# Token-major gates for the 'b' heads, rotary work first on GpSimd, and probability transposes in pairs

## The chip, the cores and the metric

The kernel runs on one core of one Trainium2 chip. The metric is the device time of one execution in microseconds; the median of several runs is given. A core has five engines with an instruction stream each: TensorE (PE in the profile, its weight loads PEld), VectorE (DVE), ScalarE (ACT), GpSimd (POOL) and SyncE (SP), which here issues nearly all DMAs.

## What is computed

One encoder layer over 1024 tokens of width 1024, in float32 accuracy. One projection gives the queries, keys, values and gates of two groups of eight heads of width 64: group 'a' is neighbourhood attention over a 16 x 64 grid, group 'b' is windowed attention with two key heads, rotary positions and a learned sink.

```python
h = jnp.einsum('bsd,de->bse', x, w_in[layer])
q_a, k_a, v_a, z_a, q_b, k_b, v_b, z_b = jnp.split(h, SPLIT_POINTS, axis=-1)
y_a = neighborhood_attention(q_a, k_a, v_a, rel_bias)          # shapes left out
qb, kb = rotary(q_b, positions), rotary(k_b, positions)
y_b = windowed_gqa_with_sink(qb, kb, v_b, sink)                # |i - j| <= 128
mixed = jnp.concatenate([y_a * jax.nn.silu(z_a), y_b * jax.nn.silu(z_b)], axis=-1)
y = jnp.einsum('bse,ed->bsd', mixed, w_out[layer])
x = layer_norm(DEEPNORM_ALPHA * x + y, ln_gain[layer], ln_bias[layer])
```

## The kernel before

**Accuracy from half precision.** Large products are made of float16 pairs. A matrix is split into a high part (rounded to float16, on ACT) and a low part (the rest, on GpSimd or DVE), and a product is three passes: high by high, high by low, low by high. A weight block therefore costs an ACT instruction (line 199) and two of GpSimd (lines 204 and 205) before TensorE can use it. `w_split(m)` orders this for the m-th half block of four rows of tiles; `w_ops[m]` is its last operation.

**Stages.** First the values are projected (lines 411 to 661). Then come 21 projections of 128 columns each, named in `ORDER`: `q`, `k`, `z` for pairs 0 to 3 of 'a' heads, `qb`, `zb` for those of 'b' heads, and `kb`. Each works in two halves of 512 tokens, 24 matmuls of 512 columns a half, with the weights as the stationary operand (`project`, line 379); its result is feature-major: features on partitions, tokens along the row. The first six (`NPRO`) run alone, from about 59 to 122 us. The other 15 are the list `fill`, spread in between the attention. Last come the output projection (line 1031; a part of it is in `fill` too) and the normalisation (`final`).

**The attention** walks through 128 units, one per step: 64 of 'b' (pair p, head j, block of 128 queries), then 64 of 'a'. A unit takes its scores (`stage_qk`, lines 816 and 817 on PE, 826 on DVE), the exponentials (`stage_exp`, line 842 on ACT), one step later the split of the probabilities (`stage_tr`, line 852 on ACT, 853 on DVE) into one of six `split` tiles and a DMA transpose from there into one of nine `tr` tiles (line 856, on SP). Four units are a quad. From six steps after a quad's last scores on, `stage_pv` multiplies its transposed probabilities with the values (line 881), 33 or 36 matmuls of 64 columns; `stage_on` divides by the sums (line 890); after the second head of a pair `stage_ot` turns the result into the feature-major form with four PE transposes (line 901), and DVE multiplies it into the gate (line 904 for 'b', 910 for 'a').

**Gates.** `evac` writes the gates into tiles `zt[e]`: with Silu on ACT for the first three of `ORDER` (line 338), with Tanh on ACT and a product on DVE for the others (lines 341 and 342). `m_queue(e)` splits the gated result of 'b' pairs (`e` 4 to 7) into `mh` and `ml` (lines 1013 on ACT, 1014 on GpSimd) from the steps `M_AT` on; `m_split` does so for 'a' in `final`.

**What sets the order.** All is written out by hand. Work that isn't part of a step waits in four queues, one per engine, as `Op`s with a priority and dependencies. `pop` takes the next ones whose dependencies were emitted in an earlier step (two steps earlier where the dependency is a DMA on SP), the lowest priority number first: two of GpSimd's in each step (`NP`), one or two of ACT's and DVE's, one of SP's. `need` emits an operation at once where the next instruction requires it. `pump_to` emits as many matmuls of `fill` as belong to the step. An engine works through what is emitted for it strictly in order.

**The rotation** (`rope`): ACT copies, DVE shuffles (line 312), and then three operations of 128x512 (lines 313 to 315), on DVE in the first six projections and on GpSimd later. `split_q` and `split_k` make the high and low parts of the rotated result (lines 259 and 265); `split_k` also copies both parts of a key head to the other 64 partitions (line 295, GpSimd).

Of the kernel before, what the change touches and what calls it, by code (L numbers as in the profile page):

```python
# [15 lines left out]
S = 1024  # L16
# [11 lines left out]
LTT, LPP, BP, BH, BR, ND, NA, NX, F1 = 1, 6, 2, 9, 5, 1, 1, 6, 0.2  # L28
NSPLIT, NP = 6, 2
ORDER = ["zb0", "z0", "zb1", "kb", "qb0", "z1", "qb1", "zb2", "qb2", "k0", "qb3", "zb3", "q0", "k1", "q1",  # L30
# [6 lines left out]
ZTAG = {"z3": "zv", "zb3": "zc", "z2": "zs", "zb1": "zd", "zb2": "ze"}  # L37
# [9 lines left out]
WO_SCALE = 55  # L47
M_AT = [105, 112, 118, 120]
# [13 lines left out]
def hybrid_block(ctx, tc, xT, x, wt, wv, wo, bias, sink, gain, lbias, cos, sin, bmask, out):  # L62
# [83 lines left out]
    class Op:  # L146
        def __init__(self, eng, fn, deps, prio):
            self.eng, self.fn, self.deps, self.step = eng, fn, [d for d in deps if d is not None], None
            self.prio, self.born, self.lag = prio, clock["step"], 2 if eng == "sp" else 0
# [17 lines left out]
    def pop(eng, n, top=1, same=False):  # L167
        q = queues[eng]
        ready = [op for op in q if op.prio <= top and all(
            d.step is not None and d.step + d.lag < clock["step"] + (same and op.prio == 0 and d.eng == "act") for d in op.deps)]  # L170
# [112 lines left out]
    def split_k(p, half, src, dep=None):  # L283
# [3 lines left out]
        eng = "pool" if dep and clock["step"] is not None else "dve"  # L287
        for j in range(2):
# [4 lines left out]
            def dup_(w, j=j, a=a, o=o):  # L293
                t = own(w, p, j)
                nc.gpsimd.tensor_copy(t[o, sl], t[a, sl])  # L295
# [4 lines left out]
            dup = [enq("pool", lambda d=dup_: d("kh"), o1, after=32 if dep else 0),  # L300
                   enq("pool", lambda d=dup_: d("kl"), o2, after=36 if dep else 0)]
            stk_ops.setdefault((p, j, half), []).extend(dup)
        return ops

    def rope(ps, half):
# [7 lines left out]
        o3 = enq(eng, lambda: mul.tensor_mul(raw, raw, tiles["cos"][:, sl]), o2, after=3)  # L313
        o4 = enq(eng, lambda: mul.tensor_mul(sw, sw, tiles["sin"][:, sl]), o2, after=3)
        o5 = enq(eng, lambda: mul.tensor_add(raw, raw, sw), o3, o4, after=4)
        return raw, o1, o5

    def evac(name, half, ps):
# [22 lines left out]
        o = enq("act", lambda: nc.scalar.activation(zt[e][:, sl], ps, AF.Tanh, scale=half_inv), prio=0)  # L341
# [5 lines left out]
    def z_col(e):  # L347
        i = 0 if e in (4, 0, 5) else 1 if e == 1 else 2
        return zc[:, i:i + 1]
# [7 lines left out]

    def project(name):
        n = ORDER.index(name)
# [397 lines left out]
    split = [ap.tile([128, 3, 2, 128], F16, name=f"split{i}", bufs=1) for i in range(NSPLIT)]  # L757
# [87 lines left out]
    def stage_tr(u):  # L845
        g, p, j, t, _ = u
        n, ch = geom(u)
        pt = st.pop((u, "p"))
        c, m = ch[0], len(ch)
        hl = split[units.index(u) % NSPLIT]  # L850
# [474 lines left out]
```

## Time and profile before

| | |
|---|---|
| median of 3 runs (lowest to highest) | 446.54 us (446.23 to 446.97) |
| profiled execution: its time | 446.49 us |
| profiled execution: its span | 444.7 us |
| mean granted TensorE clock | 0.995 |
| busy: PE, DVE, ACT, POOL | 437.5, 344.2, 308.3, 221.6 us |

The span goes from the first to the last instruction of the profiled execution. A busy time is the time in which at least one instruction of an engine was under way. Matmuls overlap: a single one of 512 columns is recorded with 379 ns, so the distance between the starts of neighbours, which the chain of waits and the timeline give, says what one costs in a row.

### The profile page before, as it was taken

The page shows a single profiled execution, that of the slowest core. Times are in us where ns is not written, and L with a number is a line of the kernel's source. Part 1 is how long each engine was busy: PE and PEld are TensorE (multiplying, and loading weights), DVE is VectorE, ACT ScalarE, POOL GpSimd, SP SyncE. Part 2 cuts the span into 40 slices and gives each one's busy share as a digit, 9 for nine tenths or more (in the row PEclk, how much of TensorE's full clock was granted, in tenths as well). Part 3 has the DMA queues.
Part 4 walks back from the last instruction along what each step waited for, and adds up shares of the span by engine and source line. Part 5 has one row for each costly group of instructions (what it writes and reads, how often), then busy time and mean ns, then how long its engine had stood idle before and what let it go on. Part 6 is the DMA issues. An engine that isn't in the chain of part 4 may idle for free.

```text
span 444.7 us, 9505 instructions
## 1 busy us (share of the span) xinstructions
PE 437.5 (98%) x3289; PEld 255.5 (57%) x3289; DVE 344.2 (77%) x849; ACT 308.3 (69%) x700; POOL 221.6 (50%) x235
## 2 busy tenths in 40 slices
PE   9999999999999999999999999999999999999994
PEld 8997754444445565655565655656555654444453
DVE  5978967438986898887988888888878837589944
ACT  5759789766499988887868887888778946302401
POOL 0110074646839558866506767765574405205740
PEclk9999999999999999999999999999999999999997
DMA  8921469984659999587978899998999998103612
GB/s 272 390 91 60 145 235 339 336 292 169 213 127 214 206 190 181 98 162 143 164 127 175 169 182 180 213 170 213 192 204 253 167 172 347 55 0 102 232 69 72
DMA packets 133841, 81.39 MB, mean 183 GB/s; under 512 B 101280, under 2 KB 113440, under 8 KB 133536
## 3 DMA queue, kind: packets, MB, share of 16 engines
q1 hardware_dynamic: 133648, 80.64, 75.4%
q8 instruction: 26, 0.43, 0.4%
q14 instruction: 23, 0.19, 0.2%
q10 hardware_dynamic: 144, 0.13, 0.1%
HBM read 50.34 MB, written 9.96 MB: 136 GB/s over the span
## 4 chain that ended last, share of the span: by engine, by line
PE 91%; DMA 3%; POOL 3%; DVE 1%; issue 1%; ACT 1%; SPq 0%; POOLq 0%; DVEq 0%; ACTq 0%
PE ps_pj L379 44%; PE ps_s L1031 9%; PE ps_s L486 6%; PE ps_t L881 6%; PE ps_pj L1031 5%; PE ps_t L1031 5%; PE ps_s L816 4%; PE ps_s L817 4%; PE ps_pj L486 3%; PE ps_t L486 3%; DMA bias<-in_bias 3%; PE ps_t L901 1%; POOL wl L205 1%; PE ps_t L412 1%; POOL ks L295 1%
## 5 line engine op out<-in xcount | busy, mean ns | idle before, releaser
L379 PE MATMUL ps_pj<-xf,wh 128*128 128x512 f16 x672 | 202.1, 379 | 0.1
L379 PE MATMUL ps_pj<-xf,wl 128*128 128x512 f16 x336 | 127.3, 379 | 0.0
L379 PEld LDWEIGHTS <-wh 128*128 128x128 f16 x672 | 63.7, 98 | 60.4 <-DVE ks L263 0.5
L842 ACT ACTIVATE ps_s<-sn,nm 128x385 f32<-128x385 f32 (+3 forms) x128 | 70.1, 548 | 25.1 <-DVE nm L826 24.6
L853 DVE SCALAR_TENSOR_TENSOR split<-ps_s,split 128x384 f16<-128x384 f32 (+2 forms) x128 | 65.7, 513 | 27.5 <-ACT split L852 25.9
L1031 PEld LDWEIGHTS <-m 128*128 128x128 f16 x432 | 40.0, 98 | 41.1 <-DVE m L939 0.2
L852 ACT ACTIVATE split<-ps_s 128x384 f16<-128x384 f32 (+2 forms) x128 | 57.8, 452 | 2.5 <-DMA tr<-split 0.2
L204 POOL TENSOR_SCALAR wr<-wr,wsc 128x512 f32<-128x512 f32 x26 | 20.6, 791 | 68.1 <-ACT wh L199 61.6
L379 PEld LDWEIGHTS <-wl 128*128 128x128 f16 x336 | 32.9, 98 | 37.4
L826 DVE CUSTOM_DVE_ANT_0 sn<-ps_s,bm,nsk 128x384 f32<-128x384 f32 (+1 forms) x64 | 40.7, 636 | 2.0 <-PE ps_s L817 1.7
L1031 PE MATMUL ps_s<-wo,m 128*128 128x512 f16 (+1 forms) x192 | 40.8, 366 | 0.0
L816 PE MATMUL ps_s<-ks,qs 128*128 128x384 f16 (+4 forms) x128 | 39.2, 306 | 0.3 <-DVE qs L263 0.3
L817 PE MATMUL ps_s<-ks,qs 128*128 128x384 f16 (+4 forms) x128 | 39.2, 306 | 0.0
L826 DVE CUSTOM_DVE_ANT_0 sn<-ps_s,bias,sg 128x264 f32<-128x264 f32 (+1 forms) x64 | 35.0, 547 | 4.5 <-issue 1.5
L881 PEld LDWEIGHTS <-tr 128*128 128x128 f16 (+1 forms) x1104 | 36.6, 98 | 2.2
L205 POOL TENSOR_TENSOR wl<-wr,wh 128x512 f16<-128x512 f32 x26 | 32.7, 1257 | 2.2
L788 POOL TENSOR_SCALAR bias<-bias,rsg 128x552 f32<-128x552 f32 (+1 forms) x24 | 19.1, 797 | 23.8 <-DMA bias<-in_bias 22.6
L295 POOL COPY ks<-ks 64x512 f16<-64x512 f16 x40 | 26.0, 661 | 7.1 <-DVE ks L263 2.8
L1086 ACT ACTIVATE sd<-mv,eps 128x1 f32<-128x1 f32 x8 | 2.4, 295 | 36.5 <-DVE mv L1084 35.2
L1031 PE MATMUL ps_pj<-wo,m 128*128 128x512 f16 (+1 forms) x144 | 26.2, 326 | 0.0
L1130 POOL TENSOR_TENSOR xr<-xr,gb 128x512 f32<-128x512 f32 x7 | 9.8, 1396 | 32.4 <-ACT xr L1127 32.4
L842 ACT ACTIVATION_READ_ACCUMULATOR ps_s<-sn,nm 128x1 f32 x128 | 24.4, 190 | 0.0
(188 smaller groups left out, 813.8 us busy)
## 6 DMA issues: line engine op xcount, KB each, us to landing
ws<-in_wt SPq DMA_DIRECT2D x15, 512.0 KB, 5.9
wr<-in_wt SPq DMA_DIRECT2D x26, 256.0 KB, 3.6
wor<-in_wo SPq DMA_DIRECT2D x22, 256.0 KB, 3.5
bias<-in_bias SPq DMA_DIRECT2D x16, 276.0 KB, 3.3
xr<-in_x SPq DMA_DIRECT2D x8, 512.0 KB, 9.6
out<-xr SPq DMA_DIRECT2D x15, 256.0 KB, 2.1
bias<-in_bias SPq DMA_DIRECT2D x8, 368.0 KB, 3.8
wvraw<-in_wv SPq DMA_DIRECT2D x9, 320.0 KB, 5.8
```

Source lines behind the costliest of these rows:

```text
L205: nc.gpsimd.tensor_sub(l, raw, h)
L295: nc.gpsimd.tensor_copy(t[o, sl], t[a, sl])
L379: nc.tensor.matmul(ps, a[:, k % 4, :], mv, start=(k == 0 and i == 0), stop=(k == KT - 1 and i == 2))
L486: nc.tensor.matmul(ps[:, :320], lh[:, ts], rh[:, cs], start=(k == ko[0] and i == 0), stop=(k == ko[-1] and i == 2))
L816: nc.tensor.matmul(ps[:, :m], q, sl[0], start=True, stop=False)
L817: nc.tensor.matmul(ps[:, :m], q, sl[1], start=False, stop=True)
L826: nc.vector.tensor_tensor_reduce(sn[:, :m], ps[:, :m], bias_t, sg[:, c:c + 1], init, op0=ALU.add, op1=ALU.min, accum_out=nm)
L842: nc.scalar.activation(pt[:, :m], sn[:, :m], AF.Exp, bias=nm, scale=-1.0, accum_out=sm[:, k:k + 1])
L852: nc.scalar.activation(hl[:, :m, 0, :c], src, AF.Copy, scale=PSCALE)
L853: nc.vector.scalar_tensor_tensor(hl[:, :m, 1, :c], src, PSCALE, hl[:, :m, 0, :c], op0=ALU.mult, op1=ALU.subtract)
L881: nc.tensor.matmul(ps[:, HD * m:HD * m + HD], a, b_, start=(i == 0), stop=(i == len(mms) - 1))
L1031: nc.tensor.matmul(ps, lh[:, ts], rh[:, cs], start=(e == EO[0] and i == 0), stop=(e == EO[-1] and i == 2))
```

## The change

**Token-major gates of 'b'.** The projections zb0 to zb3 are done with tokens on partitions: `project_rows` takes the activations as the stationary operand and the weights as the moving one, in 96 matmuls of 128 columns for each half. `stage_on` then multiplies the normalised output with its scale in one DVE operation (`scalar_tensor_tensor`), and GpSimd multiplies it into the gate. `stage_ot`, with its four PE transposes and the product on DVE, remains for 'a' alone. The gated result of 'b' is split in the token-major form and turned by one DMA transpose for each half of 512 tokens, into the gate's own tile; no other tiles are taken for `m4` to `m7`. These splits are ordered at steps 26, 42, 57 and 86.

**Order.** zb2 and zb3 change places with z0 and z1: all four zb come in the first six projections.

**Rotation.** Its operations get priority 0.45, ahead of the weight splits' 0.5, and what GpSimd makes may be used by other engines a step later than before. The copies of the keys k0 are made by DMAs on SP.

**Pairs.** Two units share a `split` tile of double width (three in place of six single ones) and a `tr` tile (four in place of nine single ones). For 'b' one DMA transpose turns both units once the second one is split; 'a' has one for each unit, as before. The `gb` and `bb` tiles of the normalisation come from another pool.

```diff
-LTT, LPP, BP, BH, BR, ND, NA, NX, F1 = 1, 6, 2, 9, 5, 1, 1, 6, 0.2
-NSPLIT, NP = 6, 2
-ORDER = ["zb0", "z0", "zb1", "kb", "qb0", "z1", "qb1", "zb2", "qb2", "k0", "qb3", "zb3", "q0", "k1", "q1",
+LTT, LPP, BP, BH, BR, ND, NA, NX, F1 = 1, 6, 2, 4, 5, 1, 1, 6, 0.2
+NSPLIT, NP = 3, 2
+ORDER = ["zb0", "zb1", "zb2", "kb", "qb0", "zb3", "qb1", "z0", "qb2", "k0", "qb3", "z1", "q0", "k1", "q1",
...
-WO_SCALE = 55
-M_AT = [105, 112, 118, 120]
+WO_SCALE = 60
+M_AT = [26, 42, 57, 86]
+POP2_AT = (105, 112)
...
-            self.prio, self.born, self.lag = prio, clock["step"], 2 if eng == "sp" else 0
+            self.prio, self.born, self.lag = prio, clock["step"], {"sp": 2, "pool": 1}.get(eng, 0)
+
+        def behind(self, eng):
+            return 0 if self.eng == eng == "pool" else self.lag
...
+        to = "sp" if p == 0 and dep is None else "pool"
...
-                nc.gpsimd.tensor_copy(t[o, sl], t[a, sl])
+                if to == "sp":
+                    nc.sync.dma_start(t[o, sl], t[a, sl])
+                else:
+                    nc.gpsimd.tensor_copy(t[o, sl], t[a, sl])
...
-        o3 = enq(eng, lambda: mul.tensor_mul(raw, raw, tiles["cos"][:, sl]), o2, after=3)
+        o3 = enq(eng, lambda: mul.tensor_mul(raw, raw, tiles["cos"][:, sl]), o2, prio=0.45, after=3)
...
+    def project_rows(name):
+        n = ORDER.index(name)
+        w_split(2 * n + 2)
+        for half in range(2):
+            ps = new_group()
+            need(w_ops[2 * n], w_ops[2 * n + 1])
+            for c in range(96):
+                t, k, i = c // 24, c // 3 % 8, c % 3
...
+                ts = slice(128 * t, 128 * t + 128)
+                h, l = parts[2 * n + k // 4]
+                a, b = ((x16h, h), (x16l, h), (x16h, l))[i]
+                nc.tensor.matmul(ps[:, ts], a[half, k][:, ts], b[:, k % 4, :], start=(c % 24 == 0), stop=(c % 24 == 23))
...
-    split = [ap.tile([128, 3, 2, 128], F16, name=f"split{i}", bufs=1) for i in range(NSPLIT)]
+    split = [ap.tile([128, 6, 2, 128], F16, name=f"split{i}", bufs=1) for i in range(NSPLIT)]
...
+        if i % 2 == 0:
+            st["tr"] = ap.tile([128, 12, 128], F16, tag="tr", name="tr", bufs=BH)
+        tr = st["tr"]
+        if g == "a":
+            nc.sync.dma_start(tr[:, 2 * o:2 * o + 6, :], hl[:, o:o + 3].rearrange("p k i c -> p (k i c)"), transpose=True)
+            st[u, "tr"] = tr[:, 2 * o:]
+            return
+        if i % 2 == 0:
+            return
+        w = 2 * (len(sizes[0][1]) + len(sizes[1][1]))
+        nc.sync.dma_start(tr[:, :w, :], hl.rearrange("p k i c -> p (k i c)")[:, :128 * w], transpose=True)
...
-        nc.vector.tensor_mul(on[g, p, h][:, :, j, :], ps[:, :4 * HD].rearrange("p (m e) -> p m e", e=HD),
-                             ri.unsqueeze(2).to_broadcast([128, 4, HD]))
+        o, src = on[g, p, h][:, :, j, :], ps[:, :4 * HD].rearrange("p (m e) -> p m e", e=HD)
+        rb = ri.unsqueeze(2).to_broadcast([128, 4, HD])
+        if g == "a":
+            nc.vector.tensor_mul(o, src, rb)
+            return
+        nc.vector.scalar_tensor_tensor(o, src, z_col(4 + p), rb, op0=ALU.mult, op1=ALU.mult)
+        z = zt[4 + p].rearrange("p (t j e) -> p t j e", j=2, e=HD)[:, 4 * h:4 * h + 4, j, :]
+        gate_ops.setdefault(4 + p, []).append(enq("pool", lambda: nc.gpsimd.tensor_mul(z, z, o), prio=0.6))
...
-        if j == 0:
+        if j == 0 or g == "b":
             return
...
-        for h in (slice(0, 512), slice(512, S)):
-            o = enq("act", lambda h=h: nc.scalar.copy(mh[e][:, h], zt[e][:, h]))
-            m_ops[e].append(enq("pool", lambda h=h: nc.gpsimd.tensor_sub(
-                ml[e][:, h], zt[e][:, h], mh[e][:, h]), o))
...
+            o = enq("act", lambda hr=hr, z=z: nc.scalar.copy(hr[:, :, 0, :], z), *gate_ops[e])
+            o = enq("pool", lambda hr=hr, z=z: nc.gpsimd.tensor_sub(hr[:, :, 1, :], z, hr[:, :, 0, :]), o)
+            m_ops[e].append(enq("sp", lambda hr=hr, out16=out16: nc.sync.dma_start(
+                out16, hr.rearrange("p t i f -> p (t i f)"), transpose=True), o))
...
-        gb, bb = gain_tile[0], zslot("bb")
+        gb, bb = gain_tile[0], big_tile("bb", (128, D), F32)
...
-            enq("sp", gain_load, *m_ops[4])
+            enq("sp", gain_load)
```

99 lines of the change are left out of this document (62 added, 37 removed).

## The prediction

> **What bounds the kernel now.** I read the page first, its engine line and the slices.
>
> ```profile
> span 444.7 us, 9505 instructions
> PE 437.5 (98%) x3289; PEld 255.5 (57%) x3289; DVE 344.2 (77%) x849; ACT 308.3 (69%) x700; POOL 221.6 (50%) x235
> PE   9999999999999999999999999999999999999994
> DMA  8921469984659999587978899998999998103612
> ```
>
> PE is busy in every slice but the last; the DMA engines come next, near full from slice 10 to 33. Busy PE is not proof of PE at its peak, so I looked for pauses in the table by stage (PE, PEld, DVE, ACT, POOL busy; clock; DMA share; GB/s) and for the pitch of matmuls in the chain of waits (start, length, what).
>
> ```profile
> 140.00:160.00 20.00, 20.00 (x188) 11.53 (x187) 16.00 (x45) 18.72 (x51) 13.23 (x13) 1.00 1.09 186
> 240.00:260.00 20.00, 19.90 (x168) 11.16 (x165) 16.83 (x47) 16.45 (x44) 14.20 (x19) 1.00 0.84 161
> 320.00:340.00 20.00, 19.75 (x171) 11.03 (x169) 15.95 (x43) 16.78 (x44) 13.94 (x17) 1.00 1.12 210
> ...
> 68.72 10.38 PE ps_pj L379 x48
> 136.30 0.96 PE ps_t L881 x33
> 434.25 2.69 PE ps_pj L1031 x48
> ```
>
> 48 matmuls of 512 columns take 10.38 us, 216.25 ns each; 33 of 64 columns take 0.96, 29.1 ns each, every one with its own stationary operand; 48 of 128 columns take 2.69, 56.0 ns each. From about 1 us to the last matmul of the projection PE runs at these pitches at a granted clock of 1.00; the two stages shown are the only ones that lack more than a few hundredths (0.10 and 0.25 us). So a PE instruction removed is time won, one added is time lost, and a pause of PE, wherever it arises, lengthens the span by itself. Everything else counts only if it makes PE pause.
>
> **PE terms.** Removed: the four transposes of each finished 'b' head pair (line 901), eight calls in all.
>
> ```profile
> 164.84 0.60 PE L901 MATMUL ps_t<-identf,on 128*128 128x128 f32 x4
> 165.17 1.11 PEld L881 LDWEIGHTS <-tr 128*128 128x128 f16 x33
> 165.28 1.13 PE L881 MATMUL ps_t<-vb,tr 128*128 128x64 f16 x33
> ```
>
> From the first transpose (164.84) to the next matmul (165.28) is 0.44 us; 8 x 0.44 = 3.5 us less. They stand in PE's own order, beside no other PE work, so all of it is on the path.
>
> Changed: the eight halves of the zb projections. Each had 24 matmuls of 512 columns; token-major it has 96 of 128. Before: 192 x 216.25 = 41.52 us. After, at the 56.0 ns of line 1031, which also loads a fresh 128x128 operand for each: 768 x 56.0 = 43.01. That is +1.5 us.
>
> Against this stands a rule. The Trainium skill, page "TensorE: Matmul & The Clock Gate", section "Back-to-back issue gap", gives about 81 ns sustained for pairs of load and matmul at 128 columns and calls the 56 an isolated figure; by it the sum would rise by 768 x 81 - 41.5 = 20.7 us in place of 1.5. The trace disagrees over 48 such pairs in a row; no run here shows 192 in a row.
>
> First start: in the old order the second weight half is first needed for its low part after 14 matmuls of 512 columns; in the new one after 14 of 128.
>
> ```profile
> 59.27 1.16 POOL L205 TENSOR_TENSOR wl<-wr,wh 128x512 f16<-128x512 f32 x1
> 59.37 0.59 PE L379 MATMUL ps_pj<-xf,wh 128*128 128x512 f16 x2
> ```
>
> The low part is ready at 60.43; PE will ask for it at 59.37 + 14 x 0.056 = 60.15. A wait of 0.3 us, where there were 2 us of slack. Later zb projections find both halves split a whole projection (10.4 us) ahead: nothing.
>
> **Work off PE.** Nearest rows:
>
> ```profile
> L1099 POOL TENSOR_TENSOR xr<-xr,gb 128x256 f32<-128x256 f32 x1 | 0.7, 728 | 0.2 <-DVE stats L1080 0.2
> L295 POOL COPY ks<-ks 64x512 f16<-64x512 f16 x40 | 26.0, 661 | 7.1 <-DVE ks L263 2.8 <-ACT ks L257 1.5 <-DMA wr<-in_wt 0.6
> L1014 POOL TENSOR_TENSOR m<-z,m 128x512 f16<-128x512 f32 x8 | 9.1, 1161 | 3.8 <-ACT m L1013 3.8
> L904 DVE SCALAR_TENSOR_TENSOR z<-ps_t,zc,z 128x512 f32<-128x512 f32 x8 | 6.0, 747 | 0.0
> L890 DVE TENSOR_TENSOR on<-ps_t,ri 128x256 f32<-128x256 f32 x32 | 13.6, 424 | 2.6 <-PE ps_t L881 1.5
> L910 DVE SCALAR_TENSOR_TENSOR z<-ps_t,zc,z 128x256 f32<-128x256 f32 x16 | 7.0, 477 | 7.8 <-PE ps_t L901 7.8
> ```
>
> DVE loses 8 x 0.747 = 6.0 us and pays about 16 x (0.477 - 0.424) = 0.8 for the scaled normalisation. GpSimd gains 16 gate multiplications at about 0.73 (11.6 us) and loses 8 copies at 0.66 (5.3 us). The eight splits of the gated values (0.61 us on ACT, 1.16 on GpSimd) are not new: they move from steps 105 to 120, where ACT and GpSimd are short (the stage that lacks 0.25 us), to steps 26 to 86. All this hides behind PE, at nothing; without that cover it would cost its own length. The relief may return up to the 0.35 us that the two stages lack; I book none.
>
> The splits now end in eight DMA transposes of 128x1024 on SP. Their results are first wanted by the output projection from step 123 on, tens of steps later: nothing on the path. But each waits on SP for GpSimd, and the next unit's transpose is queued behind it; the emission gives it two steps of lag for that. The eight copies of k0 become small DMAs in steps 25 to 40, wanted at step 64: nothing. The gain and bias tiles no longer wait for gate tiles; PE does not pause in the output stage for what lies behind them: nothing.
>
> **Pairs.** A pair's one transpose leaves when the second unit is split and moves twice the bytes.
>
> ```profile
> 139.14 2.50 SPq L856 DMA_TRANSPOSE tr<-split  x2
> 142.93 1.12 PE L881 MATMUL ps_t<-vb,tr 128*128 128x64 f16 x33
> DMA to landing us min/median/max: 2.5/3.4/6.2
> L856 SPq DMA_TRANSPOSE tr<-split x128: 1188/1212/2615, 126.1 to 361.3; - x128
> 280.00:300.00 20.00, 20.00 (x167) 11.32 (x166) 17.40 (x47) 16.42 (x43) 13.65 (x17) 1.00 1.00 194
> ```
>
> Of the two transposes from 139.14 the first is the last of the second quad of units; it leaves at 139.14, its use begins at 142.93: 3.8 us for a median landing of 3.4. The pair's data is used from the 17th of 33 matmuls, 0.5 us later, so 4.3 us are there. Bounds: a pair lands like a single (3.4) or like two in a row (6.8). At full DMA load 194 GB/s passed, so 196.6 KB more are about 1.0 us (an estimate from that row): 4.4 us. And SP, which issued without a break there at 1.21 us each, has half as many to issue, and so issues up to 1.2 us earlier. I take 0.2 us of waiting in all, near the lower bound; the upper one is a rival.
>
> **Sum.** 446.49 (profiled execution: span 444.7 and 1.8 around it) - 3.5 + 1.5 + 0.3 + 0.2 = 445.0 us. The median of the runs shown, 446.54, lies 0.05 above that execution; I leave it out. A measurement of this kernel tells about 0.2%, 0.9 us, from no change.
>
> **Rivals.**
>
> *Pairs land late* (slower).
>
> ```profile
> 234.13 2.60 SPq L856 DMA_TRANSPOSE tr<-split  x2
> 239.04 1.12 PE L881 MATMUL ps_t<-vb,tr 128*128 128x64 f16 x33
> ```
>
> Place: the value products of the 'b' quads, above all those near 143 us, where the DMA share of the stage is 1.09, and near 239 us, where the last transpose of the quad (the second of the two, 236.73 - 1.21 = 235.5) leaves 3.5 us ahead of its use. It decides from a landing of 4.3 us on. At the upper bound, 6.8, PE waits 2.5 us; having waited, it has let ACT and DVE catch up, so I count it once at each place: 445.0 + 5.0 - 0.2 = 449.8. At a landing of 5.1 the two waits have eaten the gain (444.8 + 2 x 0.8 = 446.4), at 5.8 it is 447.8. For it: DMA near full. Against: SP's relief. 18%.
>
> *The rotated queries come late* (no change).
>
> ```profile
> 139.33 2.38 POOL L265 TENSOR_TENSOR qs<-rp_raw,qs 64x512 f16<-64x512 f32 x2
> 141.79 1.27 POOL L313 TENSOR_TENSOR rp_raw<-rp_raw,cos 128x512 f32<-128x512 f32 x1
> 147.89 0.27 PE L816 MATMUL ps_s<-ks,qs 128*128 128x256 f16 x1
> 133.00:151.00 18.00, 18.00 (x178) 10.51 (x177) 13.13 (x41) 16.53 (x45) 15.82 (x14) 1.00 1.09 212
> ```
>
> GpSimd is busy for 15.8 of these 18 us. The low parts of the queries (line 265) end at 141.7 and are wanted at 147.9. With the rotation of the other half ahead of them (3 x 1.27), one weight split (1.9), a gate (0.7) and a step of lag (1.6), they end at about 149.8, unless the step order lets them in between. A wait of up to 2 us; taken as 1.3: 446.3. GpSimd has rests of 0.5 and 0.7 us there and the rotation itself begins no later, so 12%.
>
> *The transposes were not what PE waited for* (slower). In that same stage ACT is busy for 16.5 of 18 us. If ACT sets the step, PE waits the removed 3.5 us elsewhere and only the costs stay: 446.5 + 2.0 = 448.5. Against it: PE does not pause there now, and DVE has less. 10%.
>
> *Weight loads bind in long runs* (slower).
>
> ```profile
> L881 PEld LDWEIGHTS <-tr 128*128 128x128 f16 x816 | 27.6, 98 | 1.7
> ```
>
> If each of the 768 loads took its 98 ns before its matmul, they would cost 75.3 us, 33.8 more than now: 446.5 - 3.5 + 33.8 = 476.8. The pitches of 29 and 56 ns speak against it: 3%. The 81 ns of the Trainium skill's page named above would be this case at half its price.
>
> **How the numbers follow.** The sum, 57%; its own range is 444.1 (the 0.35 us given back, no wait at the first start or at the pairs), rounded down to 444.0, to 445.6. Faster by over 0.2% is below 445.6: 57%. Within 0.2%: the late queries, and late pairs at a landing near 5, 12 + 8 = 20%. Slower: 10% of late pairs, 10 and 3: 23%. The range goes from 444.0 to 448.5; outside are the worst half of the late pairs, the weight loads and some 5% below.
>
> **What would show it.** Right: line 901 with 32 transposes; the zb matmuls at 56 ns; GpSimd's second low part ahead of the first zb half with PE idle about 0.3 us; PE busy without pauses from 120 to 430 us. Wrong: PE released by the pair's DMA at the value products; line 816 released by line 265; zb matmuls above 60 ns; an idle PE in stages that have none now.

## The result and the profile after

| | before | after |
|---|---|---|
| median (lowest to highest, runs) | 446.46 us (446.22 to 446.97, 6) | 450.97 us (449.63 to 454.07, 6) |
| ratio to before, 95% interval | | 1.0106 (1.0073 to 1.0138) |
| profiled execution: time, span | 446.49, 444.7 us | 450.65, 448.8 us |

The change makes the kernel about 1% slower: 4.5 us more, where 1.5 us less was forecast, and outside the range. The medians in this document leave out one execution, of experiment 11, which took 568.43 us at a mean granted clock of 0.752.

The page after: span, busy times, PE's slices, and the head of the chain of work that ended last.

```profile
span 448.8 us, 10466 instructions
PE 436.6 (97%) x3833; PEld 276.1 (62%) x3833; DVE 341.4 (76%) x841; ACT 308.1 (69%) x700; POOL 228.4 (51%) x240
PE   9999999999999999799999999999999899999995
...
PE 76%; DVE 7%; ACT 5%; POOL 4%; issue 4%; DMA 3%; SPq 0%; DVEq 0%; POOLq 0%; ACTq 0%
```

PE has two slices under 9 that were full before (the 17th, at 180 us, and the 32nd, at 350 us). The chain now passes through DVE, ACT, POOL and DMA for 19% of the span, where it was 8% before: PE waits for them more often. The table by stage (columns as in the prediction) says where, and its last row how much:

```profile
160.00:180.00 20.00, 19.35 (x161) 10.33 (x157) 16.35 (x47) 16.76 (x42) 15.47 (x15) 1.00 0.94 188
180.00:200.00 20.00, 17.67 (x174) 10.23 (x175) 15.99 (x47) 15.22 (x39) 13.73 (x15) 1.00 0.77 144
...
340.00:360.00 20.00, 18.82 (x193) 11.48 (x192) 15.24 (x45) 13.71 (x36) 2.33 (x3) 1.00 1.07 202
sum 240.00, PE 234.28 PEld 133.90 DVE 195.00 ACT 194.17 POOL 156.34; mean PE 19.52 PEld 11.16 DVE 16.25 ACT 16.18 POOL 13.03
```

The same stages of the kernel before:

```profile
sum 240.00, PE 239.64 PEld 137.54 DVE 199.14 ACT 197.44 POOL 148.40; mean PE 19.97 PEld 11.46 DVE 16.59 ACT 16.45 POOL 12.37
```

From 120 to 360 us PE lacks 5.7 us where it lacked 0.4. What it waits for, in the view of waits (engine, tile and line, releaser: us in total, times, longest):

```profile
PE ps_s L856 <- POOL qs L269: 3.0, 1, 3.0
...
PE ps_t L934 <- DMA tr<-split: 1.4, 3, 1.0
...
PE ps_s L856 <- DVE qs L267: 0.6, 1, 0.6
PE ps_pj L419 <- DVE ks L267: 0.5, 2, 0.3
PE ps_pj L419 <- DVE qs L267: 0.2, 1, 0.2
PE ps_pj L389 <- POOL wl L209: 0.2, 1, 0.2
```

(Line 856 was 816: scores; 934 was 881: value products; 419 was 379; 267 and 269 were 263 and 265: low parts of the feature-major results, and of the rotated ones; 389 is the matmul of `project_rows`.) Before, the same view had one such row of 0.3 us. Idle time is counted from the modelled end of the matmul before; by the distance of starts, less the pitch, a pause is a little longer. Summed that way from the first zb matmul to the last matmul of the output projection (before the change, from the first matmul of line 379), the pauses are 7.35 us after and 0.69 before. The rest of that stretch, PE's own work, is 374.71 us after and 376.65 before: 1.9 less, where 2.0 (-3.5 + 1.5) was forecast. The stretch begins 0.2 us later, and what follows it is 0.8 us shorter (7.2 us against 8.0). So 6.7 - 1.9 + 0.2 - 0.8 = 4.2 us, and the two spans (448.8 and 444.7) differ by 4.1; the medians differ by 4.5. The forecast of PE's work held, and new pauses made the loss.

**The 3.0 us pause** comes at unit 32, the first of pair 2, the third of the four pairs of 'b' heads. The timeline of PE:

```profile
178.97 0.38 PE L419 MATMUL ps_pj<-xf,wl 128*128 128x512 f16 x1
182.33 0.28 PE L856 MATMUL ps_s<-ks,qs 128*128 128x256 f16 x1 [2.98 <-POOL qs L269]
```

And what GpSimd did meanwhile, with one operation of DVE put ahead (start, length, engine and line, operation; in brackets idle time before it and releaser):

```profile
165.12 0.72 DVE L322 STREAM_SHUFFLE rp_sw<-rp_raw 128x512 f32<-128x512 f32 x1
...
163.75 0.72 POOL L952 TENSOR_TENSOR z<-z,on 128x256 f32<-128x256 f32 x1 [2.69 <-DVE on L950]
165.98 1.28 POOL L323 TENSOR_TENSOR rp_raw<-rp_raw,cos 128x512 f32<-128x512 f32 x1 [1.51 <-DVE sn L861]
...
171.70 0.72 POOL L952 TENSOR_TENSOR z<-z,on 128x256 f32<-128x256 f32 x1
172.39 2.27 POOL L1078 TENSOR_TENSOR hr<-z,hr 128x512 f16<-128x512 f32 x2
174.63 1.26 POOL L323 TENSOR_TENSOR rp_raw<-rp_raw,cos 128x512 f32<-128x512 f32 x1
175.85 1.26 POOL L324 TENSOR_TENSOR rp_sw<-rp_sw,sin 128x512 f32<-128x512 f32 x1
177.19 1.26 POOL L325 TENSOR_TENSOR rp_raw<-rp_raw,rp_sw 128x512 f32<-128x512 f32 x1
178.44 0.69 POOL L208 TENSOR_SCALAR wr<-wr,wsc 128x512 f32<-128x512 f32 x1
179.21 1.15 POOL L209 TENSOR_TENSOR wl<-wr,wh 128x512 f16<-128x512 f32 x1
180.32 0.73 POOL L952 TENSOR_TENSOR z<-z,on 128x256 f32<-128x256 f32 x1
181.12 3.60 POOL L269 TENSOR_TENSOR qs<-rp_raw,qs 64x512 f16<-64x512 f32 x3
```

The low part that unit 32 needs (line 269) stands last: behind the rotation of the other half (lines 323 to 325, 3.8 us), a weight split, a gate product (line 952), and the moved splits of gated values (line 1078, 2.3 us). At 163.75 a gate product has also held GpSimd still for 2.7 us, because it was emitted in the same step as the normalisation on DVE (line 950) that it needs. The pause at unit 32 did not grow by it: the rotation of the first half, behind this gate product, needs the shuffle on DVE (line 322), which ends at 165.84, and so GpSimd idled again until 165.98. From there to the low part GpSimd has no rest.

Two things set unit 32 apart from units 16 and 48, where PE doesn't pause. The queue from the first rotation (line 323) to the low part is 15.1 us long and not 13.2 or 13.1; the two splits of line 1078, 2.3 us, stand in it only here. And that rotation starts 13.2 us before PE wants the unit, and not 15.2 or 14.7.

### The profile page after: what moved, and what is told of

It reads as the page before. It is cut to its first block, busy times and chain, and to the rows that moved or that the text cites. A ratio compares the mean times of both kernels' runs of the same rounds, so it can differ in the third digit from the quotient of the medians.

```text
span 448.8 us, 10466 instructions
## 1 busy us (share of the span) xinstructions
PE 436.6 (97%) x3833; PEld 276.1 (62%) x3833; DVE 341.4 (76%) x841; ACT 308.1 (69%) x700; POOL 228.4 (51%) x240
## 4 chain that ended last, share of the span: by engine, by line
PE 76%; DVE 7%; ACT 5%; POOL 4%; issue 4%; DMA 3%; SPq 0%; DVEq 0%; POOLq 0%; ACTq 0%
PE ps_pj L419 27%; PE ps_pj L389 9%; PE ps_s L1096 9%; PE ps_s L526 6%; PE ps_t L1096 5%; PE ps_pj L1096 5%; PE ps_t L934 5%; PE ps_pj L526 3%; PE ps_s L856 3%; PE ps_s L857 3%; DVE split L896 2%; DMA tr<-split 2%; PE ps_t L526 2%; ACT split L895 1%; DVE qs L267 1%
## 5 line engine op out<-in xcount | busy, mean ns | idle before, releaser
L419 PE MATMUL ps_pj<-xf,wh 128*128 128x512 f16 x544 | 164.0, 379 | 0.7 <-DVE ks L267 0.5
L419 PE MATMUL ps_pj<-xf,wl 128*128 128x512 f16 x272 | 103.1, 379 | 0.0
L419 PEld LDWEIGHTS <-wh 128*128 128x128 f16 x544 | 51.3, 98 | 46.6 <-DVE ks L267 1.0
L419 PEld LDWEIGHTS <-wl 128*128 128x128 f16 x272 | 26.6, 98 | 30.0
L389 PEld LDWEIGHTS <-xf 128*128 128x128 f16 x768 | 43.2, 98 | 0.6 <-issue 0.3
L389 PE MATMUL ps_pj<-wh,xf 128*128 128x128 f16 x512 | 43.4, 219 | 0.0
L389 PE MATMUL ps_pj<-wl,xf 128*128 128x128 f16 x256 | 43.2, 219 | 0.2 <-POOL wl L209 0.2
L828 POOL TENSOR_SCALAR bias<-bias,rsg 128x552 f32<-128x552 f32 (+1 forms) x24 | 19.0, 794 | 33.8 <-DMA bias<-in_bias 22.1
L1096 PEld LDWEIGHTS <-m 128*128 128x128 f16 x216 | 20.2, 98 | 21.4 <-DVE m L998 0.2
L1096 PEld LDWEIGHTS <-z 128*128 128x128 f16 x216 | 20.0, 98 | 19.7
```

Source lines behind the costliest of these rows:

```text
L389: nc.tensor.matmul(ps[:, ts], a[half, k][:, ts], b[:, k % 4, :], start=(c % 24 == 0), stop=(c % 24 == 23))
L419: nc.tensor.matmul(ps, a[:, k % 4, :], mv, start=(k == 0 and i == 0), stop=(k == KT - 1 and i == 2))
L1096: nc.tensor.matmul(ps, lh[:, t, :], rh[:, cs], start=(e == EO[0] and i == 0), stop=(e == EO[-1] and i == 2))
```

## The experiments

The theory after the first reading: PE's terms are right, and the change adds three waits. GpSimd stands still in front of operations that wait for DVE, and has the wrong order; SP stands in front of the new DMA transposes until GpSimd is done; SP is full in the 'a' stage. The rival: the order of the whole is so tight that a pause taken away in one place comes back in another. Edits are against the kernel after, unless said otherwise; each ratio is to the kernel before, on the same chip. Numbers 12 to 15 ran as four together, in this order, and so did 6, 8, 17 and 18: that is what "the second of these four" and the like mean in the expectations.

### The order on GpSimd

**1. Rotation part undone** (priority and lag as before the change).

```diff
-self.prio, self.born, self.lag = prio, clock["step"], {"sp": 2, "pool": 1}.get(eng, 0)
+self.prio, self.born, self.lag = prio, clock["step"], 2 if eng == "sp" else 0
...
-o3 = enq(eng, lambda: mul.tensor_mul(raw, raw, tiles["cos"][:, sl]), o2, prio=0.45, after=3)
+o3 = enq(eng, lambda: mul.tensor_mul(raw, raw, tiles["cos"][:, sl]), o2, after=3)
...
```

> The changed kernel with its rotation part undone: the three GpSimd operations of the rotation have their old priority 1, and GpSimd's results may be used in the next step. Theory 'order': the 3.1 us pause before the scores of unit 32 comes from the order on GpSimd (the other half's rotation, one weight split and the gate splits ahead of the low parts of the queries, 8.7 us in the trace of the changed kernel). The low parts then follow the first half's rotation after one weight split and a gate product, so they end near 175 us, 4 us before they are wanted: no pause there, time 450.97 - 3.1 = 447.9 us. Theory 'load': the pause comes from the work that GpSimd was given in addition (gate products, splits at step 26); then the order changes little, at least 1.5 us of pause stay, and the time is 449.4 us or more.

Measured: 451.31 us, 1.0121 (1.0074 to 1.0168). A miss: the pause at unit 32 went, but PE then waited for DVE at the scores (2.8 us) and for DMAs at the value products (2.6 us). These waits are those of the profiled execution, which at 455.13 us is the longest of the four.

**2. Only the lag of GpSimd's results undone** (the first line of that diff).

> The changed kernel with one part of the rotation undone: GpSimd's results may be used in the next step again; the rotation keeps its priority of 0.45. Theory 'order': the other half's rotation (3.8 us) and a weight split (1.9 us) stay ahead of the low parts, but the gate splits (2.3 us) now come behind them, so the low part ends near 179.3 us and about 0.2 us of pause stay: time 448.1 us. Theory 'load': the work is the same, the pause stays above 1.5 us.

Measured: 450.69 us, 1.009 (1.0057 to 1.0123). The pause at unit 32 went: the low part still stands behind the other half's rotation, but now ahead of the splits of gated values and of a gate product, and ends at 178.7 us, just in time. Pauses at the value products of 'b' took its place. The timelines of SP and then of PE show where:

```profile
208.00 1.75 SPq L908 DMA_TRANSPOSE tr<-split  x1
214.28 1.23 SPq L1079 DMA_TRANSPOSE z<-hr  x1
215.62 1.40 SPq L908 DMA_TRANSPOSE tr<-split  x1
```

```profile
228.35 0.70 PE L934 MATMUL ps_t<-vb,tr 128*128 128x64 f16 x18 [1.84 <-DMA tr<-split]
```

SP ends an issue at 209.75 and then stands for 4.5 us in front of a transpose of gated values (line 1079), whose split GpSimd makes from 213.1 on; the next pair of units (line 908) is behind it. That pair was split by 211.1; it leaves 4.5 us late and lands at 219.15, and PE pauses 0.5 us for it. ACT waits for the same landing, because it needs the `split` tile again (1.0 us), and waits for the next one at 224.2 (1.3 us): the delay is handed on through the three tiles. The pair that PE misses at 228.35 itself left as soon as it was split (222.8) and took until 228.31 to land, so how much of the 1.84 us comes from SP's standing is not shown. In the kernel after no such pause is seen; PE comes 3 us later there.

**3. Only the priority of the rotation undone** (the rest of that diff).

> The changed kernel with the other part undone: the rotation has its old priority 1, the step of lag stays. Theory 'order': the gate splits (2.3 us) and a weight split (1.9 us) are ahead of the low parts, the other half's rotation is behind, so the low part ends near 177.8 us, 1.4 us early: no pause at unit 32, time 447.9 us. If the lag alone were the cause, the pause would stay at 3 us and the time near 451.

Measured: 455.18 us, 1.019 (1.0165 to 1.0214). The pause at unit 32 went, as the theory of the order had it, but the time is a miss: with the lag kept and the rotation behind the weight splits, the low part of the second half of the queries comes later still, and PE waits for line 269 once, 5.1 us, at unit 36. So the priority helps the rotation, but leaves the queries' splits behind it. Between the two profiled executions, this one and that of the kernel after, only 2.1 us of the 5.0 is more waiting; the rest goes with the granted clock (last section).

**4. Splits of the gated values later** (`M_AT = [36, 52, 66, 86]`).

> The changed kernel with the splits of the gated values of the first three 'b' pairs ordered ten steps later (steps 36, 52, 66 and 86 in place of 26, 42, 57 and 86); rotation as in the changed kernel. Theory 'order': 2.3 us of what is ahead of the low parts at unit 32 goes, 0.8 us of pause stay there, time 448.7 us, unless the splits find another place to be in the way. Theory 'load' gives the same at unit 32; with the runs that leave the work and change the order this tells how the 3.1 us divide.

Measured: 450.87 us, 1.0099 (1.0068 to 1.013). A miss: the pause is still 2.5 us. With the splits away GpSimd stands for DVE instead (0.9 us ahead of the rotation, 0.7 ahead of a gate product), and the low part begins at 180.3 in place of 181.1.

**5. Gate products two steps after their normalisation.**

```diff
-gate_ops.setdefault(4 + p, []).append(enq("pool", lambda: nc.gpsimd.tensor_mul(z, z, o), prio=0.6))
+made = Op("dve", None, [], 1)
+made.step = clock["step"] + 1
+gate_ops.setdefault(4 + p, []).append(enq("pool", lambda: nc.gpsimd.tensor_mul(z, z, o), made, prio=0.6))
```

> The changed kernel with one change: a gate product of GpSimd is emitted two steps after the normalisation (line 950) that makes its input, and not in the same step. In the trace of the changed kernel GpSimd stood 20.2 us in all in front of the gate products, waiting for DVE, with all its other work behind it. Theory 'GpSimd blocked': without these waits the rotation and the low parts of the queries are earlier by 2 to 3 us, the pause of 3.1 us before unit 32 goes, and as in the run with the old lag the value products of 'b' may then pause 1 to 3 us because the pairs' transposes leave late: 448 to 449.5 us. Theory 'load' (the added work itself): GpSimd still ends the low parts late, the pause stays above 1.5 us, time 449.4 us or more.

Measured: 449.02 us, 1.0051 (1.0034 to 1.0068). GpSimd's waits for the normalisation, after and here:

```profile
POOL z L952 <- DVE on L950: 20.2, 8, 6.8
```

```profile
POOL z L954 <- DVE on L950: 2.5, 1, 2.5
```

17.7 us of standing still are gone, but PE gains only about 2 us, and unit 32 still waits 1.7 us. Nor does this show that the standing made the pause. The rotation starts no earlier than in the kernel after (165.98), since it needs the shuffle:

```profile
166.04 1.28 POOL L323 TENSOR_TENSOR rp_raw<-rp_raw,cos 128x512 f32<-128x512 f32 x1 [4.21 <-DVE sn L861]
```

What got shorter is the queue: with their gate products later, the splits of gated values start at 182.4 in place of 172.4, behind the low part, which begins at 179.9 in place of 181.1. What the standing is worth by itself is not separated.

**6. Only the splits of the queries ahead of the rotation** (gate products as in the kernel after).

```diff
 def split_q(...):
-    prio = 0 if dep is None else 1
+    prio = 0 if dep is None else 0.4
```

> The changed kernel, in which only the splits of the queries go ahead of the rotation by priority (0.4 against 0.45) on ACT and GpSimd; the gate product stays behind the normalisation in the same step. Theory 'the order on GpSimd': the pause of 3.1 us at line 856 (unit 32) falls below 1 us; pauses at the value products of 'b' may appear instead, as they did whenever that pause went: 448 to 450. Rival 'the gate products block GpSimd': the pause stays at 1.5 to 3 us, since GpSimd still stands about 20 us in all: 450 to 451.

Measured: 448.01 us, 1.0042 (1.0027 to 1.0057); 3.0 us of the 4.5 come back with this number alone (it also orders the high parts on ACT). GpSimd in it:

```profile
172.53 2.29 POOL L1078 TENSOR_TENSOR hr<-z,hr 128x512 f16<-128x512 f32 x2
174.89 2.38 POOL L269 TENSOR_TENSOR qs<-rp_raw,qs 64x512 f16<-64x512 f32 x2
177.35 1.27 POOL L323 TENSOR_TENSOR rp_raw<-rp_raw,cos 128x512 f32<-128x512 f32 x1
```

Two low parts (line 269) now stand ahead of the other half's rotation and end at 177.3, and the pause at unit 32 is gone. GpSimd still stood 2.4 us for a normalisation at 163.9. The pause is thus shown to come from the order. Waits for DMAs at the value products took a part back: 2.6 us in place of 1.4.

### The queue of SP

**7. Pairs of 'b' undone** (`if g == "a":` becomes `if True:`).

> The changed kernel with the pairs undone: each unit of 'b' has its own DMA transpose again (the tiles stay double). Theory 'pairs help or are neutral': SP has 32 issues of 1.2 us more between 126 and 240 us, in front of which the transposes of the gated values wait too; 451 to 453 us. Rival 'pairs cause the loss': the time falls by 2 us or more, to 449 us or less.

Measured: 454.02 us, 1.0164 (1.0145 to 1.0183): 3.1 us slower than the kernel after. PE waits 3.9 us for DMAs at the value products, 2.5 more than in the kernel after. Not all of the 3.1 need be the pairs: the tiles stay double here (four `tr` tiles of two units in place of nine of one), and in the profiled execution the granted clock is 0.50 for 3.4 us after the pause at unit 32.

**8. Pairs alone, in the kernel before** (its `stage_tr` replaced by the new one; three double `split` tiles, four double `tr` tiles).

> The kernel before with the pairs alone: tiles of double width, one DMA transpose for two 'b' units, one each for 'a'; gates, order and rotation as before. Theory 'pairs cost nearly nothing': no pause at the value products of 'b' and a time within 0.5 us of the kernel before (446.1 to 447.1). Rival 'pairs land late': pauses at the value products near 143 and 239 us, 0.5 to 2 us each: 447.5 to 450.

Measured: 446.62 us, 1.0011 (0.9997 to 1.0025): no difference. PE nowhere waits for a pair. In the trace, an issue of SP for one unit of 'a' (line 862) and for a pair (line 868), lowest, median and highest ns:

```profile
L862 SPq DMA_TRANSPOSE tr<-split x64: 1209/1218/1883, 245.4 to 359.9; - x64
L868 SPq DMA_TRANSPOSE tr<-split x32: 1255/1427/2163, 127.0 to 242.6; - x32
```

Up to twice the data costs SP 17% more time, so pairs save SP two fifths.

**9. Token-major gates alone** (experiment 1's diff, and no pairs; the new order of the projections, the copies of k0 on SP and the double tiles stay).

> The changed kernel with the rotation part undone (priority and lag of GpSimd's results as before) and one DMA transpose for each unit: of the change stay the token-major gates with their splits and DMA transposes, and the order of the projections that belongs to them. Theory 'the gates bring new work to GpSimd and SP, whose waits cost more than the 2.0 us that PE saves': slower than the kernel before by 5 to 9 us, 451.5 to 455.5, with pauses at the scores and at the value products. Rival 'the loss comes from the new order of the rotation': 445 to 447, near the prediction's sum.

Measured: 457.81 us, 1.0268 (1.0236 to 1.0299): 11.2 us slower, more than either theory gave. What PE waits for most in it:

```profile
PE ps_t L934 <- DMA tr<-split: 8.1, 7, 1.5
PE ps_s L856 <- DVE split L896: 2.1, 3, 1.3
```

And SP:

```profile
184.02 1.80 SPq L1079 DMA_TRANSPOSE z<-hr  x1
185.94 1.22 SPq L902 DMA_TRANSPOSE tr<-split  x1
187.20 0.58 SPq L301 DMA_DIRECT2D ks<-ks  x1
188.26 1.35 SPq L902 DMA_TRANSPOSE tr<-split  x1
189.72 1.24 SPq L1079 DMA_TRANSPOSE z<-hr  x1
```

SP stands in front of the first transpose of gated values until 184, and then goes from one issue to the next: the transposes of the units, those of the gated values, and the eight copies of k0 that the change gave it. An issue, which ends 1.3 us after its unit is split when SP is free, ends 7.1 us after it at 210.5 us, and still 4.3 at 241.2. Against experiment 1, which has the same gates and old rotation but pairs, the pairs are worth 457.8 - 451.3 = 6.5 us. In this change they pay for the gates.

**10. 'a' units in pairs too** (the `if g == "a"` block is left out). In the kernel after, the last split of gated values falls into the 'a' stage. Its SP there, and PE later:

```profile
292.95 1.23 SPq L1079 DMA_TRANSPOSE z<-hr  x1
294.29 1.31 SPq L902 DMA_TRANSPOSE tr<-split  x1
295.69 1.26 SPq L1079 DMA_TRANSPOSE z<-hr  x1
```

From here on SP is behind: its issues end up to 6.9 us after their split, where in this stage of the kernel before it is up to 5.4.

```profile
357.31 0.44 PE L934 MATMUL ps_t<-va,tr 96*128 96x64 f16 x9 [0.95 <-DMA tr<-split]
```

> The changed kernel with one change: the units of 'a' too are turned in pairs, so that SP issues 32 transposes less between 245 and 366 us. Theory 'SP is full there': SP issues without a break from 292 us on and its transposes leave 2 to 5 us after their split is done; the value products pause 0.4 us at 304 and 1.5 us at 356. With pairs SP has 32 x 1.2 = 38 us less to issue; the pauses go, 450.97 - 1.9 = 449.0 us. Rival 'pairs are long': the second unit of a pair then lands later by 0.6 us against 1.4 to 2.9 us of slack; pauses of the value products stay or grow, 451 us or more.

Measured: 448.68 us, 1.005 (1.0028 to 1.0072): 2.3 us back, as the theory had it. PE's waits for DMAs fall from 1.4 to 0.7 us, which is only a part of that; unit 32 still waits 3.0. The profiled execution, 450.17 us, is the longest of the five: after the pause at unit 32 its granted clock is 0.51 from 182.2 to 185.6 us.

**11. Experiment 5, and the transposes of gated values five steps after their split** (`o.lag = 4` on the split).

> As the run before it, and the DMA transposes of the gated values are emitted on SP five steps after GpSimd's split and not two. Theory 'SP blocked': in the run with the old lag SP stood 4.5 us in front of such a transpose (5.6 and 5.5 us in all for two of them), and the next pair's transpose, behind it, left late; the value products paused 2.0 us at 226 us. Without that wait the pauses of the value products of 'b' go: 1 to 2 us less than the run with the gate lag alone, 446.5 to 448 us. Rival 'pairs are long': the pause comes from the double length of a pair's transfer; then this run equals the other within 0.5 us.

Measured: 452.75 us, 1.0139 (1.0107 to 1.0171). A miss: no longer waiting for GpSimd, these transposes now come when the 'a' units begin, and PE waits 4.3 us for DMAs. SP's time there is what lacks, not only its standing: between 249 and 258 us its issues end 4 to 5 us after their split.

### All together

**12. Gate products later, lag undone** (5 and 2 together).

> The changed kernel with two edits: the gate product of GpSimd is emitted two steps after the normalisation it needs, and what GpSimd makes may again be used in the next step (lag as before the change). Theory 'GpSimd in order': the 3.1 us pause at line 856 (unit 32) and the small pauses at the same line go, because GpSimd neither waits for the normalisation nor has the other half's rotation in front of the low part; what stays are the pauses in 'a' (about 2.3 us) and at the first zb half (0.3): 447.5 to 448.5. Rival 'one pause hides another': with PE on time the transposes of the gated values, which wait on SP for GpSimd, stand in front of pair transposes, and PE pauses at the value products of 'b' (line 934 with a DMA as releaser) for 2 to 3 us: 449.5 to 451.

Measured: 448.74 us, 1.0049 (1.0031 to 1.0067). Between the two theories: no wait at unit 32, but 3.8 us for DMAs at the value products, three quarters of it in 'b', as the rival said. Here SP's part is plain: the pair that PE misses longest, at 220.2, was split by 211.5, but its issue ends at 218.1, behind both transposes of gated values, in front of which SP had stood up to 4.5 us for GpSimd.

**13. The same with pairs in 'a', and the passes of the first zb half in another order.**

```diff
 t, k, i = c // 24, c // 3 % 8, c % 3
+if n == 0 and half == 0 and t == 0:
+    k, i = (c // 2 % 8, c % 2) if c < 16 else (c - 16, 2)
```

> The first of these four kernels, and besides: 'a' units are also turned in pairs by one DMA transpose (half as many issues of SP there), and in the first 24 matmuls of the first zb half the two passes that need only high parts of the weights come first, so that the second low part is wanted 6 matmuls (0.34 us) later. Theory 'each wait has its own cause': the pauses of 'a' shrink from 2.3 to about 1.0 us and the one at the first zb half goes; with no pause at unit 32: 444.8 to 446.3, at or below the kernel before. Rival 'one pause hides another': 448 or more, with pauses at line 934 in 'b'.

Measured: 447.06 us, 1.0007 (0.9993 to 1.0021). Level with the kernel before, and again between the two theories. The 0.3 us at the first zb half is gone; 3.6 us of waits for DMAs remain.

**14. The same, last split of gated values at step 76** (`M_AT = [26, 42, 57, 76]`).

> The second of these four kernels with the last of the four splits of the gated values ordered at step 76 in place of 86, that is, its two DMA transposes go to SP some ten steps earlier, before SP has to serve the densest part of 'a'. Theory 'SP is put behind by these two transposes': the remaining pauses at the value products of 'a' from 350 us on (about 1 us) shrink by half or more: 0.4 to 0.8 us below the second kernel. Rival 'the transposes of a itself fill SP': no difference beyond 0.3 us.

Measured: 447.16 us, 1.0012 (0.9995 to 1.003). No difference, as the rival had it; the pause at 354 us went, and one of 1.0 came at 288.

**15. Number 13 with the lag kept and the queries' splits at 0.4** (5, 6, 10 and the passes).

> The second of these four kernels, but the one-step lag of GpSimd's results is kept, and instead the splits of the queries go ahead of the rotation by priority (0.4 against 0.45) on ACT and GpSimd. Theory 'GpSimd in order': what counts is only that the low part of the queries stands ahead of the other half's rotation, so the pause at unit 32 goes here too: within 0.8 us of the second kernel. Rival 'the lag itself holds the chain back': the pause at line 856 stays above 1 us and the time is 1 to 2 us above the second kernel.

Measured: 446.42 us, 1.0001 (0.9989 to 1.0013), the lowest median of all, and no different from the kernel before. What is left:

```profile
PE ps_s L858 <- DVE split L898: 0.6, 2, 0.4
PE ps_s L858 <- DVE qs L267: 0.5, 1, 0.5
PE ps_pj L421 <- DVE ks L267: 0.5, 2, 0.3
```

No wait for GpSimd, and none for a DMA that reaches 0.3 us. By distances of starts 3.2 us of pauses remain, against 0.7 before, and PE's work is 2.05 us less. With 0.1 us more ahead of it and 0.4 less behind, this gives the 0.2 us by which the spans differ (444.9 and 444.7); the median is 0.1 lower.

**16. Number 15 with one transpose for each unit.**

> The version that came out level with the kernel before (gate product two steps later, queries' splits by priority 0.4, passes of the first zb half reordered), with one DMA transpose for each unit in both groups. Theory 'SP lacks the time for the eight transposes of gated values and for one transpose per unit': pauses at the value products come back, 2 to 4 us in all: 448.5 to 450.5. Rival 'with the waits on GpSimd away SP has room': within 1 us of that version.

Measured: 453.3 us, 1.0144 (1.0122 to 1.0166). PE waits 7.6 us for DMAs, in a profiled execution of 456.54 us, the longest of the four, whose granted clock is 0.50 for 3.4 us after each of two such waits (from 233.1 and from 362.8 us). Pairs, here in both groups, are worth 6.9 us, more than expected; a part of it may be that clock, or the double tiles.

**17. and 18. Number 15 with the third split of gated values at step 66, and then with the scaling of the output weights at step 55 as well** (`WO_SCALE = 55`).

> The fourth kernel of the last four (gate product two steps later, queries' splits by priority 0.4, pairs also in 'a', passes of the first zb half reordered), with the third split of gated values ordered at step 66 in place of 57, so that its two ACT copies of 0.6 us no longer lie between 233 and 238 us. Theory 'ACT and DVE set the step there': the pauses at the scores between 236 and 241 us (1.1 us together) shrink by half or more: 0.4 to 1.0 us below that kernel. Rival 'the removed transposes took their cover with them, wherever the splits lie': the pauses stay or move by a few us: within 0.3 us of it.

> The third of these four kernels with the scaling of the output weights ordered at step 55, as in the kernel before, in place of 60, so that its last reduction on DVE (0.68 us) and the five small operations after it (0.9 us in all) lie earlier than 225 us. Theory 'ACT and DVE set the step there': a further 0.2 to 0.6 us less. Rival as for the third: within 0.3 us of it.

Measured: 446.59 us, 0.9997 (0.9985 to 1.0009), and 448.98 us, 1.0052 (1.003 to 1.0074). In the first of the two the pauses between 236 and 241 us went, but one of 1.0 us for a DMA came at 225 us, and the time stayed, as the rival had it. The second is a plain miss: at step 55 the reductions on DVE that the scaling needs are not done, and PE itself waits for them:

```profile
PE ps_t L1030 <- DVE wom L1021: 3.6, 1, 3.6
```

## Why the prediction was wrong, step by step

**PE sets the span, and every pause lengthens it**: right; the sum above closes on the difference of the spans to 0.1 us. But a pause can also cost more than its length (last section), which I had not reckoned with.

**PE terms, -3.5 and +1.5**: right. Line 962 has only the 32 transposes of 'a', and the zb halves run at 56 ns a matmul:

```profile
69.54 10.74 PE ps_pj L389 x192
...
L962 PE MATMUL ps_t<-identf,on 128*128 128x128 f32 x32 | 4.8, 273 | 0.0
```

192 matmuls in a row with a fresh operand each take 10.74 us, 55.9 ns apiece. By this, the 81 ns that the Trainium skill gives in "TensorE: Matmul & The Clock Gate", section "Back-to-back issue gap", does not hold here, and the rival of binding weight loads is out. (The price that I worked out from that figure, 20.7 us, is three fifths of that rival's 33.8, not half.)

**First start, +0.3**: right (0.2 in the waits, 0.3 by starts). Number 13 shows that it can be had for nothing.

**"All this hides behind PE, at nothing"**: this step failed, and with it the sentence on SP after it ("the emission gives it two steps of lag for that"), which was costed at nothing. I had counted GpSimd's busy time, 11.6 us in and 5.3 out, and its length was right. But GpSimd takes its queue in order, as its timelines show, and what decides is what stands ahead of an operation that PE wants. The queries' low part stood behind the other half's rotation, a weight split, a gate product and the splits of gated values: 3.0 us of pause, gone when one priority number put it ahead (6). SP has to issue the new transposes between those of the units, and stands in front of some until GpSimd is done; with one transpose for each unit that comes to 3 to 7 us more (7, 9, 16). That GpSimd stands 20.2 us for DVE in front of gate products is seen; what this costs by itself is not shown, and at 163.75, ahead of unit 32, it cost nothing. The gates alone cost 11.2 us with 2.0 us less work for PE: 13 us of waits in the place of nothing.

**Pairs, +0.2**: about right for their own cost (no difference in the kernel before; no wait for a pair in the kernel after), and wrong in what they do beside the gates: they give 3.1 us in the kernel after, 6.5 and 6.9 in the versions without the pause at unit 32 (with the limits named there). I had noted that SP would have half as many to issue, and took it for a bonus of 1.2 us on landing, not for what SP needs to carry the new transposes.

**Copies of k0 on SP, nothing**: not so in the gates alone, where they fill SP from 187 us on; with pairs no trace shows a price. They weren't tried by themselves.

**The rivals.** *The rotated queries come late* was the true mechanism, line 816 (now 856) released by line 265 (now 269). I priced it at unit 16 (147.9 us), at 1.3 us, and gave it 12%. It came at unit 32, for 3.0 us: only there the splits of gated values stand ahead of the low part, and the first rotation starts 2 us later against PE, because its input from DVE is not there. My sum held the other half's rotation, one weight split, one gate and the step of lag, and neither of these. *Pairs land late*: did not happen in the kernel after, where a pair lands in 3.8 us at the median and I had 4.3 to spare; in 2, 12 and 13 PE does wait for pairs. (The DMA engines, which I called near full from slice 10 on, stand at 4 to 6 tenths in slices 10 to 12 and at 5 in slice 17.) *The transposes were not what PE waited for*: true in a small part. The waits of 0.7 us at line 419 and of 0.6 at line 856 for DVE are nearly absent before, and the best version keeps such waits. Why they grew is not shown; that PE now arrives 0.4 us earlier is one guess.

**What stays open**: in the version level with the kernel before, why new pauses come. PE's work is 2.05 us less there, and 2.5 us more of pauses eat it. They are small and most sit at DVE, but moving two of their loads away (17 and 18) only moved the pauses. In these kernels a pause taken away was given back elsewhere again and again (1, 2, 11, 12, 14, 17).

## What to carry to other kernels

Where an engine's work is off the critical path, don't price it by its busy time: write down for each operation that the bounding engine waits for what stands ahead of it in its queue, and what each of those waits for. An operation that depends on another engine's work of the same step holds its whole queue; ask what the work behind it is waiting for before you blame it. Put what is wanted soonest first. Count the issues on a queue of DMAs as well as the bytes: the cheap part of a change (here the pairs) may be what pays for the dear one.

## What the runs showed of the hardware beyond the expected

An issue of a DMA transpose of two units keeps SP 1.43 us at the median, that of one unit 1.22 us, so SP's time goes by the number of transposes far more than by their size. The transposes of gated values, of 128x1024, take a median of 1.25 us of SP in the kernel after:

```profile
L1079 SPq DMA_TRANSPOSE z<-hr x8: 1231/1245/1627, 176.6 to 295.7; - x8
```

A pause of PE can cost more than its length. In experiment 3, after the 5.1 us of waiting, the granted clock (here 0.50, behind the busy times) is at half for 6.8 us, and matmuls of 512 columns start about 425 ns apart, not 216:

```profile
190.80:197.60 6.80, 5.89 (x44) 3.40 (x45) 2.31 (x6) 3.46 (x8) 3.86 (x4) 0.50 0.39 72
```

Half of the 5.89 us in which PE was busy there is 2.9 us (an estimate); with 2.1 us more waiting it makes up the 5.0 us by which the span is longer than in the kernel after. The profiled executions of experiments 1, 7, 10, 11 and 16 have such stretches of 3.4 us, each after a pause of 1.5 to 3.3 us. The length of the pause alone does not tell: after the 3.0 us in the kernel after and after the 3.6 us in experiment 18 the clock stayed at 1.00.
